# Modulation sums spread over other stages, and other banks for one inverse, in a two-layer hybrid decoder trunk

## The chip, the cores and the metric

The kernel runs on one core of a Trainium2 chip. The metric is the device time of one execution in microseconds, from start to end; the median of several executions counts. Inputs and outputs are in the chip's memory, all in 32-bit floats.

## The reference

Two layers work on 256 tokens of width 2048. Each layer first makes six modulation rows from the condition `c`, then a mixer (half the width is sliding-window attention, half an RWKV-7 recurrence), then a SwiGLU feed-forward; both end in a layer norm.

```python
for l in range(DEPTH):
    mod = einsum('bd,de->be', silu(c), w_ada[l]) + b_ada[l]
    sh_m, sc_m, gt_m, sh_f, sc_f, gt_f = rows 0 to 5 of mod
    u = x * (1 + sc_m) + sh_m
    proj = u @ w_in[l]
    y_attn = sliding_window_attention(...)
    y_rwkv = rwkv7_group(...)
    x = layer_norm(alpha * x + gt_m * (concat(y_attn, y_rwkv) @ w_out[l]))
    u = x * (1 + sc_f) + sh_f
    gate, up = split(u @ w_gate_up[l])
    x = layer_norm(alpha * x + gt_f * ((silu(gate) * up) @ w_down[l]))
```

In the recurrence a state S of 64 by 64 per head follows `S = S*w + (S a) b' + v k'`, and the output is `S r`.

## The kernel before

**Weights.** All large products run in 32-bit floats rounded for TensorE, each weight split into a high and a low part, so that a product takes three matmuls. `steps` (line 364) streams a weight matrix: one DMA puts 1024 columns into a `raw` buffer (4 of them), ScalarE casts it to `hi` (line 380), VectorE subtracts to get `lo` (line 381, two buffers), and `stream` or `tstream` does the matmuls (lines 402 to 405, 414 to 416). One such step is 512 KB. All DMAs of the kernel are issued by one queue, SP's, in order.

**Modulation.** The product of `silu(c)` with `w_ada` is no matmul: `ada_steps` (line 244) makes half a row (1024 columns) in 16 steps. Each loads 512 KB of `w_ada` into an `ast` buffer (two of them, line 253), and VectorE adds it, scaled, to the sum `aacc` (line 257; the first of the 16 is line 255). Then TensorE transposes the sum in 8 blocks (line 277), ScalarE sums them, and a gate's half row (rows 2 and 5) is transposed once more and written to memory. Layer 0's first two rows are made ahead of everything; the other 20 half rows come from one generator, `ada_rest`, in a fixed order: 2, 4 and 3, 5 of layer 0; 1 and 0, 2, 4 and 3, 5 of layer 1. Here one of its 16 additions is called a modulation step.

**What sets when a modulation step comes.** Three kinds of numbers advance the generator. `pump`, called once per weight step, advances it by a pace: `AP` in the mixer, `AO` from the output projection to the first part of the feed-forward, `AF_` behind that, each with one number per layer. `recur` advances it by `AR` at each of four chunks. The operations of the attention (`a`, `b`, `c`) advance it by `AA` each. Where a row is needed and not there, `need` runs the generator until it is. Before the change 18 of the 20 half rows are begun in layer 0; the last two, row 5 of layer 1, which the last gate needs, fall into the second mixer.

**The mixer.** Eight pairs of heads are worked on in four recurrent groups of two. For group g the order string `ORDER[l]` (line 36) lists: `D` decays, `R` projection, `A` preparation, `I` the inverse of a triangular matrix, `C` the recurrence over four chunks, `E` closing; then the attention (`Q` its projection, `a` rotation, `b` weights, `c` gathering) and the output projection's first 1024 columns (`w`, `z`). The inverse (`invert`, line 722) goes through memory: GpSimd inverts 16 by 16 blocks, which are written to `tinv` and read back as `tm`; then two levels merge blocks, each with a transpose on VectorE (line 745), matmuls into a bank `m1` (line 749), a masked multiply `yx` (line 752), matmuls into `m2` (line 756) and an addition (line 757).

**Banks.** `bank` (line 88) gives out PSUM banks: tag `cb` is a ring of two, used by the recurrence (line 760) and the closing (line 836); tag `mb` alternates between `m0` and `m1`, one bank each, used by the preparations, the transposes and the modulation sums. Four more banks, `acc`, hold products and the attention.

**Order on the engines.** The program is written in the order of these strings and calls. A scheduler then lays every engine's instructions out by its own estimate of time, and each engine takes its list in order. Changed numbers of `AP` to `AF_` so move instructions everywhere behind the first place they touch, not only the modulation steps.

## Time and profile before

| | |
|---|---|
| median of three executions | 2698.06 us (2688.91 to 2700.31) |
| the profiled execution | 2694.28 us |
| its span, first to last instruction | 2692.6 us |
| mean granted clock of TensorE | 0.965 |
| busy in the span: TensorE, VectorE, ScalarE, GpSimd | 93%, 68%, 44%, 5% |
| moved by DMA | 637.49 MB, mean 237 GB/s |

The engines are named PE (TensorE), PEld (its weight loads), DVE (VectorE), ACT (ScalarE), POOL (GpSimd) and SP (the engine that issues DMAs). A busy time is the time in which at least one instruction of the engine ran. A wait is the idle time of an engine before an instruction, put down to the instruction or DMA that came last before it. L257 is line 257. A tile's name, as `aacc<-ast,cond,aacc`, gives what is written and what is read. The clock is the share of 2.4 GHz that was granted to TensorE. Layer 0's mixer lies at about 135 to 600 us, its feed-forward up to 1400; layer 1's mixer from 1446 to about 1860, its feed-forward behind that.

### The profile page before, as it was taken

How to read it: one execution, taken by the hardware profiler on the slowest of the kernel's cores; microseconds unless marked ns; L12 is line 12 of the kernel's file. 1: busy time of each engine (PE TensorE's matmuls, PEld its weight loads, DVE VectorE, ACT ScalarE, POOL GpSimd, SP SyncE). 2: the span in 40 equal slices, each digit the busy share in tenths (PEclk: the TensorE clock that was granted, in tenths of full speed). 3: DMA queues.
4: the chain of work that ended last, by engine and by line, in shares of the span. 5: the costliest groups of instructions: out<-in, count | busy, mean ns of one | idle time of the engine just before them, and what ended most of it. 6: DMA issues, size and time to landing. Idle time of an engine off the chain costs nothing.

```text
span 2692.6 us, 41752 instructions
## 1 busy us (share of the span) xinstructions
PE 2501.1 (93%) x15325; PEld 2093.1 (78%) x15325; DVE 1841.0 (68%) x2469; ACT 1188.3 (44%) x2029; POOL 135.0 (5%) x355
## 2 busy tenths in 40 slices
PE   3788998788999999999999999979899999999997
PEld 2687886567888888888889877867688888888887
DVE  6866767979877777777788677555764545545456
ACT  2364452435444444444445544534444444344442
POOL 1002112000000000000000022110000000000000
PEclk9789998899999999999999999989999999999999
DMA  9968668688998888889878586424756656666654
GB/s 315 381 188 253 198 191 238 180 317 296 353 330 309 297 303 312 293 295 308 308 263 304 174 259 188 117 72 144 253 172 188 190 186 196 195 189 189 193 188 149
DMA packets 351999, 637.49 MB, mean 237 GB/s; under 512 B 75894, under 2 KB 142898, under 8 KB 350258
## 3 DMA queue, kind: packets, MB, share of 16 engines
q1 hardware_dynamic: 351794, 634.82, 71.6%
q8 instruction: 120, 1.97, 0.3%
q14 instruction: 85, 0.70, 0.1%
HBM read 622.08 MB, written 12.62 MB: 236 GB/s over the span
## 4 chain that ended last, share of the span: by engine, by line
PE 68%; DMA 8%; DVE 6%; ACT 2%; issue 1%; POOL 1%; SPq 0%; DVEq 0%; POOLq 0%; ACTq 0%
PE acc L403 19%; PE acc L402 19%; PE acc L405 19%; DMA ast<-in_w_ada_dram 3%; DVE aacc L257 2%; PE acc L414 2%; PE acc L415 2%; PE acc L416 2%; DVE lo L381 1%; DMA raw<-in_w_gate_up_dram 1%; PE mb L1225 1%; DMA raw<-in_w_out_dram 1%; DMA yf<-yd 1%; PE mb L277 1%; ACT pr L947 0%
## 5 line engine op out<-in xcount | busy, mean ns | idle before, releaser
L380 ACT CAST hi<-raw 128x1024 fp32r<-128x1024 f32 (+2 forms) x728 | 758.5, 1044 | 1110.8 <-PE acc L405 833.1
L381 DVE TENSOR_TENSOR lo<-raw,hi 128x1024 fp32r<-128x1024 f32 (+2 forms) x728 | 880.2, 1212 | 519.8 <-PE acc L403 347.1
L403 PE MATMUL acc<-lo,u 128*128 128x512 f32 x1568 | 513.4, 395 | 11.9 <-DVE lo L381 11.8
L405 PE MATMUL acc<-hi,u 128*128 128x512 f32 x1568 | 505.8, 391 | 0.0
L257 DVE SCALAR_TENSOR_TENSOR aacc<-ast,cond,aacc 128x1024 f32<-128x1024 f32 x300 | 384.1, 1280 | 127.8 <-DMA ast<-in_w_ada_dram 126.6
L402 PE MATMUL acc<-hi,u 128*128 128x512 f32 x1568 | 457.2, 393 | 0.9 <-ACT u L360 0.5
L403 PEld LDWEIGHTS acc<-lo,u 128*128 128x128 f32 x1568 | 293.8, 189 | 76.4 <-DVE lo L381 16.2
L402 PEld LDWEIGHTS acc<-hi,u 128*128 128x128 f32 x1568 | 294.9, 188 | 63.4 <-ACT sg L1218 0.9
L405 PEld LDWEIGHTS acc<-hi,u 128*128 128x128 f32 x1568 | 295.2, 188 | 61.8 <-issue 0.5
L403 PE MATMUL acc<-lo,ht 128*128 128x512 f32 (+1 forms) x720 | 243.6, 377 | 3.0 <-DVE lo L381 2.9
L405 PE MATMUL acc<-hi,ht 128*128 128x512 f32 (+1 forms) x720 | 242.2, 375 | 0.0
L414 PE MATMUL acc<-u,hi 128*128 128x256 f32 x720 | 206.1, 293 | 14.0 <-ACT hi L380 14.0
L402 PE MATMUL acc<-hi,ht 128*128 128x512 f32 (+1 forms) x720 | 217.0, 376 | 0.0
L415 PE MATMUL acc<-u,hi 128*128 128x256 f32 x720 | 204.5, 291 | 0.0
L416 PE MATMUL acc<-u,lo 128*128 128x256 f32 x720 | 193.1, 294 | 7.1 <-DVE lo L381 7.1
L403 PEld LDWEIGHTS acc<-lo,ht 128*128 128x128 f32 x720 | 135.0, 188 | 29.3 <-DVE lo L381 5.6
L414 PEld LDWEIGHTS acc<-u,hi 128*128 128x128 f32 x720 | 141.9, 197 | 19.3 <-ACT hi L380 14.9
L405 PEld LDWEIGHTS acc<-hi,ht 128*128 128x128 f32 x720 | 135.6, 188 | 24.2
L402 PEld LDWEIGHTS acc<-hi,ht 128*128 128x128 f32 x720 | 134.8, 188 | 24.4
L415 PEld LDWEIGHTS acc<-u,hi 128*128 128x128 f32 x720 | 141.7, 197 | 2.6 <-issue 1.6
L416 PEld LDWEIGHTS acc<-u,lo 128*128 128x128 f32 x720 | 133.8, 197 | 11.6 <-DVE lo L381 9.0
L1067 POOL TENSOR_TENSOR brs<-brs,mhalf 128x1 f32<-128x1 f32 x8 | 7.6, 955 | 1698.7 <-DVE brs L1066 772.1
(349 smaller groups left out, 2901.1 us busy)
## 6 DMA issues: line engine op xcount, KB each, us to landing
ast<-in_w_ada_dram SPq DMA_DIRECT2D x368, 512.0 KB
raw<-in_w_gate_up_dram SPq DMA_DIRECT2D x704, 256.0 KB
raw<-in_w_down_dram SPq DMA_DIRECT2D x176, 512.0 KB
raw<-in_w_in_dram SPq DMA_DIRECT2D x82, 512.0 KB
raw<-in_w_out_dram SPq DMA_DIRECT2D x64, 512.0 KB
raw<-in_w_in_dram SPq DMA_DIRECT2D x120, 256.0 KB
ast<-in_w_ada_dram SPq DMA_DIRECT2D x32, 256.0 KB
lnw<-in_ln_w_dram SPq DMA_DIRECT2D x4, 1024.0 KB
```

Source lines behind the costliest of these rows:

```text
L257: ins = V.scalar_tensor_tensor(acc, t, cond[:, j:j + 1], acc, ALU.mult, ALU.add)
L277: PE.transpose(b[:, i * P:(i + 1) * P], blocks[q + i], ident)
L380: S.copy(h, fl)
L381: ins = V.tensor_tensor(r, fl, h.bitcast(F32), ALU.subtract)
L402: PE.matmul(bt, lhsT=xh, rhs=hi[:, c0:c0 + w], start=st, stop=False)
L403: PE.matmul(bt, lhsT=xh, rhs=lo[:, c0:c0 + w], start=False, stop=False)
L405: PE.matmul(banks[t][q][:, 0:w], lhsT=xl, rhs=hi[:, c0:c0 + w], start=False, stop=sp_)
L414: PE.matmul(bt, lhsT=hi[:, c0:c0 + w], rhs=xh, start=st and opens, stop=False)
L415: PE.matmul(bt, lhsT=hi[:, c0:c0 + w], rhs=xl, start=False, stop=False)
L416: PE.matmul(bt, lhsT=lo[:, c0:c0 + w], rhs=xh, start=False, stop=sp_ and closes)
L1067: G.tensor_tensor(rs[:, 0:1], rs[:, 0:1], mhalf[:, 0:1], ALU.pow)
L1225: PE.transpose(b[:, i * T + t * P:i * T + (t + 1) * P], hh[t][:, (2 * k2 + i) * P:(2 * k2 + i + 1) * P], ident)
```

## The change

Layer 1's numbers fall: no modulation step comes from the recurrence (7 before) or the attention (45), the mixer's pace goes from 0.3 to 0.2 and that from the output projection on from 2.9 to 0. Layer 0's feed-forward goes from 0.75 to 0.8. And the four merge banks of the inverse of the fourth recurrent group of layer 1 come from `mb` in place of `cb`.

```diff
--- before.py
+++ after.py
@@ -46,13 +46,13 @@
 LAG = 2
 WB = (4, 3, 2)
 RED = 1
-AR = (3, 7)
-AA = (1, 45)
-AP = (0.65, 0.3)
-AO = (1.1, 2.9)
-AF_ = (0.75, 0.55)
+AR = (3, 0)
+AA = (1, 0)
+AP = (0.65, 0.2)
+AO = (1.1, 0.0)
+AF_ = (0.8, 0.55)
 COEX = (0, 0)
-IB = 'cb'
+IB = (('cb',) * 4, ('cb', 'cb', 'cb', 'mb'))
 EB = 'cb'
 CE = (0, 1, 0, 0)
 NE = (1,)
@@ -743,14 +743,14 @@
             for level in range(2):
                 yt = pb.tile([P, 2 * NCH, CH], F32, tag="ytr", name="ytr", bufs=1)
                 V.transpose(yt.rearrange("p e s -> p (e s)"), tm.rearrange("p e s -> p (e s)"))
-                m1 = bank("m1", IB)
+                m1 = bank("m1", IB[l][g])
                 for e in range(2 * NCH):
                     for i in I2:
                         PE.matmul(m1[BH[i], e * CH:(e + 1) * CH], lhsT=st[i]["am"][e // NCH][BH[i], e % NCH, 0:CH], rhs=yt[BH[i], e, :],
                                   start=True, stop=True)
                 yx = pb.tile([P, 2 * NCH, CH], F32, tag="yx", name="yx", bufs=1)
                 V.tensor_mul(yx, m1.rearrange("p (e s) -> p e s", s=CH), mmask[:, level:level + 1, :].to_broadcast([P, 2 * NCH, CH]))
-                m2 = bank("m2", IB)
+                m2 = bank("m2", IB[l][g])
                 for e in range(2 * NCH):
                     for i in I2:
                         PE.matmul(m2[BH[i], e * CH:(e + 1) * CH], lhsT=yx[BH[i], e, :], rhs=tm[BH[i], e, :], start=True, stop=True)
```

**First place: VectorE in the second mixer**, around an inverse's second step. `bv` ends a preparation, `lw` and `ar` belong to decays and preparation, `xk` and `xr` to the shifted projections, `ytr` is the inverse's transpose. Before (here from the third group's preparation, around the second group's inverse):

```order
L455 SCALAR_TENSOR_TENSOR xk<-acc,par_132,xk 128x255
L257 SCALAR_TENSOR_TENSOR aacc<-ast,cond,aacc 128x1024
L720 TENSOR_TENSOR bv<-bnb,vx 128x256
L662 SCALAR_TENSOR_TENSOR ar<-xk,der_134,e_15512 128x4x64
L381 TENSOR_TENSOR lo<-raw,hi 128x1024
L455 SCALAR_TENSOR_TENSOR xr<-acc,par_132,xr 128x255
L257 SCALAR_TENSOR_TENSOR aacc<-ast,cond,aacc 128x1024
L662 SCALAR_TENSOR_TENSOR ar<-xk,der_134,e_15525 128x4x64
L745 STREAM_TRANSPOSE ytr<-tm 128x512
L455 SCALAR_TENSOR_TENSOR xr<-acc,par_132,xr 128x255
L675 TENSOR_TENSOR ar<-xr,e_15512 128x4x64
```

Now, around the transpose of the first group's inverse:

```order
L662 SCALAR_TENSOR_TENSOR ar<-xk,der_134,e_14424 128x4x64
L720 TENSOR_TENSOR bv<-bnb,vx 128x256
L611 MEMSET e_15901 128x4
L745 STREAM_TRANSPOSE ytr<-tm 128x512
L455 SCALAR_TENSOR_TENSOR xr<-acc,par_132,xr 128x255
L381 TENSOR_TENSOR lo<-raw,hi 128x1024
L675 TENSOR_TENSOR ar<-xr,e_14424 128x4x64
L611 MEMSET e_15914 128x4
L381 TENSOR_TENSOR lo<-raw,hi 128x1024
L752 TENSOR_TENSOR yx<-m_14757,mmask 128x512
```

The modulation steps that stood between these instructions are gone from this stretch; the `lo` splits follow each other more closely. In the whole mixer 32 steps of lines 255 and 257 stood behind the first value-residual instruction (line 545); now 9 stand there, 2 behind the coefficients of the next part (line 1089) and 9 in the feed-forward.

**Second place: VectorE at the layer norm that ends layer 0.** `tp` is the feed-forward's last piece times its gate, `z` the residual stream, `bst`, `bmv` and `brs` its statistics; lines 1264 to 1267 and 1064 to 1078 are done once per half of the tokens. Before:

```order
L1264 TENSOR_TENSOR tp<-acc,gtf 128x512
L1265 SCALAR_TENSOR_TENSOR z<-z,tp 128x512
L1267 BN_STATS bst<-z 128x6
L1064 BN_AGGR bmv<-bst 128x2
L1066 TENSOR_SCALAR brs<-bmv 128x1
L1072 SCALAR_TENSOR_TENSOR brs<-bmv,brs 128x1
L1078 TENSOR_SCALAR z<-z,brs 128x512 x2
L1264 TENSOR_TENSOR tp<-acc,gtf 128x512
L1265 SCALAR_TENSOR_TENSOR z<-z,tp 128x512
L1267 BN_STATS bst<-z 128x6
L1064 BN_AGGR bmv<-bst 128x2
L1066 TENSOR_SCALAR brs<-bmv 128x1
```

Now (ahead of the first row stand line 1264 and one more modulation step):

```order
L257 SCALAR_TENSOR_TENSOR aacc<-ast,cond,aacc 128x1024
L1265 SCALAR_TENSOR_TENSOR z<-z,tp 128x512
L1267 BN_STATS bst<-z 128x6
L1064 BN_AGGR bmv<-bst 128x2
L1066 TENSOR_SCALAR brs<-bmv 128x1
L1264 TENSOR_TENSOR tp<-acc,gtf 128x512
L1072 SCALAR_TENSOR_TENSOR brs<-bmv,brs 128x1
L1265 SCALAR_TENSOR_TENSOR z<-z,tp 128x512
L1078 TENSOR_SCALAR z<-z,brs 128x512 x2
L257 SCALAR_TENSOR_TENSOR aacc<-ast,cond,aacc 128x1024
L1267 BN_STATS bst<-z 128x6
L257 SCALAR_TENSOR_TENSOR aacc<-ast,cond,aacc 128x1024
```

One step stood ahead of the chain. Now three stand in it, one of them before the first half's line 1265 and two around the second half's statistics. On the DMA queue the four loads that feed these and the next step stand in one row, where single ones stood between the weights.

**Third place: TensorE at the attention's start in the second mixer.** `qr` is the rotated query, `ob` and `db` are the third group's recurrence, `m` is a merge bank of the fourth inverse, `qT` enters the attention's scores. Before:

```order
L906 MATMUL acc<-ident,qr 128x128 x3
L825 MATMUL db<-state_13876,mt 64x64
L906 MATMUL acc<-ident,qr 128x128 x2
L811 MATMUL ob<-state_13875,rh 64x128 x2
L814 MATMUL ob<-uv,am 64x64 x4
L749 MATMUL m_17408<-ytr,am 64x64 x7
L906 MATMUL acc<-ident,qr 128x128
L749 MATMUL m_17408<-ytr,am 64x64
L906 MATMUL acc<-ident,qr 128x128 x3
L749 MATMUL m_17408<-ytr,am 64x64 x2
L906 MATMUL acc<-ident,qr 128x128 x2
L925 MATMUL acc<-qT 128x256 x4
```

Now:

```order
L906 MATMUL acc<-ident,qr 128x128 x4
L811 MATMUL ob<-state_13932,rh 64x128 x2
L814 MATMUL ob<-uv,am 64x64 x4
L845 MATMUL gb<-gda,g2a 128x256
L846 MATMUL gb<-gdb,g2b 128x256
L845 MATMUL gb<-gda,g2a 128x256
L846 MATMUL gb<-gdb,g2b 128x256
L906 MATMUL acc<-ident,qr 128x128 x2
L749 MATMUL m_17347<-ytr,am 64x64 x16
L906 MATMUL acc<-ident,qr 128x128 x6
L925 MATMUL acc<-qT 128x256 x4
L756 MATMUL m_17366<-tm,yx 64x64 x7
```

The first merge's 16 matmuls, which stood in four pieces between the transposes of `qr`, now stand in one.

## Rows read from the trace of the kernel before

**Rows 1.** Busy us (count) by stage of PE, PEld, DVE, ACT, POOL; clock, DMA share, GB/s.
```profile
650.00:1340.00 690.00, 685.37 (x3102) 563.73 (x3101) 525.17 (x502) 317.28 (x478) 0.00 (x0) 1.00 0.89 309
1446.00:1655.00 209.00, 194.52 (x1695) 169.79 (x1695) 151.13 (x218) 105.19 (x211) 30.36 (x68) 0.97 0.74 232
1655.00:1764.00 109.00, 108.18 (x1159) 91.15 (x1160) 63.67 (x110) 48.97 (x95) 22.37 (x65) 0.98 0.47 128
1764.00:1830.00 66.00, 48.97 (x520) 37.01 (x522) 43.13 (x164) 28.64 (x104) 2.79 (x5) 0.82 0.18 52
1950.00:2620.00 670.00, 670.00 (x3012) 555.10 (x3011) 341.44 (x341) 283.58 (x310) 0.00 (x0) 1.00 0.59 189
```

**Rows 2.** The same view, line 257 alone: DVE busy us (count), clock, DMA share, GB/s.
```profile
650.00:1340.00 690.00, 190.48 (x149) 1.00 0.89 309
...
1446.00:1655.00 209.00, 47.38 (x37) 0.97 0.74 232
```

**Rows 3.** Waits of VectorE, 1446 to 1655 us: total, times, longest.
```profile
DVE aacc L257 <- DMA ast<-in_w_ada_dram: 28.9, 16, 6.9
```

**Rows 4.** Timeline of VectorE at the three places: start, length, instruction, idle before it.
```profile
1568.95 1.28 DVE L257 SCALAR_TENSOR_TENSOR aacc<-ast,cond,aacc 128x1024 f32<-128x1024 f32 x1 [4.93 <-DMA ast<-in_w_ada_dram]
...
1585.85 1.28 DVE L257 SCALAR_TENSOR_TENSOR aacc<-ast,cond,aacc 128x1024 f32<-128x1024 f32 x1 [3.35 <-DMA ast<-in_w_ada_dram]
...
1650.65 1.28 DVE L257 SCALAR_TENSOR_TENSOR aacc<-ast,cond,aacc 128x1024 f32<-128x1024 f32 x1 [6.86 <-DMA ast<-in_w_ada_dram]
...
1654.12 1.22 DVE L381 TENSOR_TENSOR lo<-raw,hi 128x1024 fp32r<-128x1024 f32 x1
```

**Rows 5.** Waits of TensorE, 1560 to 1655 us.
```profile
PE ab L599 <- DVE e L611: 3.0, 1, 3.0
PE acc L403 <- DVE lo L381: 2.2, 1, 2.2
```

**Rows 6.** Timeline of TensorE behind the last of the three.
```profile
1655.39 0.80 PE L403 MATMUL acc<-lo,u 128*128 128x512 f32 x1 [5.32 <-DVE lo L381]
...
1657.27 0.63 PE L402 MATMUL acc<-hi,u 128*128 128x512 f32 x1
1657.69 0.63 PE L403 MATMUL acc<-lo,u 128*128 128x512 f32 x1
...
1658.93 0.39 PE L403 MATMUL acc<-lo,u 128*128 128x512 f32 x1
1659.16 0.39 PE L405 MATMUL acc<-hi,u 128*128 128x512 f32 x1
```

**Rows 7.** Timeline of the DMA queue ahead of the last of the three.
```profile
1645.00 1.29 SPq L738 DMA_DIRECT2D tinv<-ttl  x2
1646.38 0.57 SPq L253 DMA_DIRECT2D ast<-in_w_ada_dram  x1
```

**Rows 8.** The view of rows 1 for two stretches at the lower granted clock.
```profile
1587.20:1594.00 6.80, 6.48 (x47) 5.30 (x48) 4.63 (x9) 1.93 (x7) 0.00 (x0) 0.50 0.97 342
...
1788.60:1805.60 17.00, 15.51 (x114) 11.61 (x115) 12.30 (x60) 8.85 (x37) 0.00 (x0) 0.50 0.00 0
```

**Rows 9.** Waits of TensorE, 1400 to 1690 us, the layer norm's.
```profile
PE mb L354 <- DVE z L1078: 4.0, 1, 4.0
```

**Rows 10.** Waits of TensorE and of VectorE in feed-forward 0.
```profile
PE acc L403 <- DVE lo L381: 3.9, 7, 1.2
...
DVE aacc L257 <- DMA ast<-in_w_ada_dram: 60.0, 48, 3.6
```

**Rows 11.** The view of rows 1 for the slice with the most bytes in feed-forward 0.
```profile
673.00:740.30 67.30, 66.23 (x298) 53.89 (x297) 55.00 (x55) 32.41 (x50) 0.00 (x0) 1.00 0.97 353
```

**Rows 12.** Waits of TensorE, 1690 to 1960 us, the attention's and the inverse's.
```profile
PE acc L906 <- DVE qr L899: 6.0, 1, 6.0
PE acc L925 <- DVE mx L932: 5.1, 1, 5.1
...
PE m L749 <- DVE es L942: 0.3, 1, 0.3
```


## The prediction

> **What bounds the kernel now.** I read the busy time of each engine by stage first. In the feed-forward of layer 0 (650 to 1340 us) TensorE is busy 685.37 of 690 us, in that of layer 1 (1950 to 2620) 670 of 670 [rows 1]: these stages are TensorE's, and work put on another engine there costs only what makes TensorE wait. The second mixer is different. In its first part (1446 to 1655 us) TensorE is busy 194.52 of 209 us, in its second part (1655 to 1764) 108.18 of 109, in the attention at its end (1764 to 1830) 48.97 of 66. What is to be seen: the first part loses 14.5 us, the second 0.8.
>
> The second view splits off the modulation steps, VectorE's multiply-adds of line 257: 37 stand in the first part and 149 in layer 0's feed-forward [rows 2]; the last of all starts at 1650.65 [rows 4], so the second part has none. The third view, of waits, says what they do in the first part: 16 of the 37 hold VectorE until their piece of `w_ada` lands, 28.9 us in all, 6.9 the longest [rows 3]. VectorE works in order, so all that stands behind such a step waits too. The timelines show three places where TensorE pays. At 1568.95 a step starts after 4.93 us of idle VectorE, and the `lo` split behind it releases TensorE after 2.2 us. At 1585.85 one starts after 3.35 us, the `bv` multiply behind it reads a preparation bank, and TensorE's next decay matmul has waited 3.0 us (the releaser named is a tiny instruction behind the multiply). At 1650.65 one starts after 6.86 us, the `lo` split comes at 1654.12, and TensorE has stood 5.32 us [rows 4 to 6]. The cause of the last lies on the DMA queue: it wrote the inverse's result, `tinv`, at 1645.00, and the step's load, which stands behind that write, left at 1646.38 [rows 7].
>
> **The change part by part.** Total work is the same: 20 half rows of 16 modulation steps, some of which move on VectorE and in the DMA queue, and their sums with them. By the order of the program 32 steps (two opening ones of line 255 among them) stand behind the first value-residual instruction of layer 1 before, and 9 of them before the output projection now. Of the other 23, 12 go ahead into layer 0's feed-forward and the start of the second projection, 2 to the output projection, 9 to layer 1's feed-forward.
>
> *Taken out of the second mixer.* The three stalls are 2.2 + 3.0 + 5.32 = 10.5 us. After a stall TensorE's clock stays at its lower level, 1.2 of 2.4 GHz, for a while: after the last one, matmuls of 512 columns follow each other every 0.42 us, and every 0.23 once it is back [rows 6], so 45% of the time is lost. TensorE worked so from 1655.39 to 1658.93, which loses 1.6 us. From 1587.20 to 1594.00, behind the middle stall, the granted clock is 0.50 with TensorE busy 6.48 of 6.80 us [rows 8], which loses 2.9 at the most. I take 10.5 + 4.5 = 15.0 us out. Bounds: 9.1, if the middle stall and its clock stay because the inverse and the decay matmuls wait for something else there, and 17.5, if all but what the second part shows of the 14.5 us goes: 209 x 0.8 / 109 = 1.5 would be left, 13.0 saved, and the 4.5 of the clock with it come on top.
>
> *Left in it.* Nine steps remain in the mixer and two in the output projection. Priced as those of before, 15.0 / 37 = 0.41 us each, they cost 11 x 0.41 = 4.5 us. Bounds: 0, if none has to wait, and 10.5 if they fall on such places again.
>
> *The layer norm between the layers.* Three steps now stand inside its chain on VectorE, where one stood ahead of it (second place of the order). A step takes 1.28 us and the next instruction starts 1.2 us after it [rows 4]. TensorE already waits 4.0 us there for `z` [rows 9], so nothing covers them: 3 x 1.2 = 3.6 us at the most, less a little, since a multiply now fills the wait for GpSimd's power; I take +3.5. Their loads are four in a row on the DMA queue, each needing one of two buffers. Bounds: 0, if the first falls in time in which TensorE still multiplies, and 3.6 + 4.93 + 6.86 = 15.4, if two of them wait as the two longest above.
>
> *Layer 0's feed-forward.* It holds 12 steps more. TensorE lost 3.9 us there to the `lo` splits with 149 steps [rows 10], so 12 x 3.9 / 149 = 0.3 us. VectorE is busy 525 of 690 us [rows 1], 15 us more fits. Bounds 0 and 35 (the last rival). The HBM Reference of the Trainium skill, Specifications (TRN2), speaks against it: it gives a core an effective 358 GB/s, and the busiest slice here already moves 353 [rows 11]. Scaled by 318 / 309 for the 12 loads of 0.52 MB that slice would want 363, and by the page it would last 1.4%, some 0.9 us, longer. The rows of this trace decide otherwise: at 353 GB/s TensorE was busy 66.23 of 67.30 us.
>
> *Layer 1's feed-forward.* Nine steps of 1.28 us and one half row's sum (9 transposes) fall into 670 us in which VectorE is busy 341 and the DMA engines 59% [rows 1]. Nothing waits there now. I take 0; if the cover were gone, one wait as the longest seen, 5.3 us.
>
> *The banks of the fourth inverse.* In layer 1 its four merges take the two banks of the preparations in place of the ring that the recurrence and the closing use. Its matmuls lose 0.3 us to waits now [rows 12], so I price the swap by that. On TensorE the first merge now stands in one piece between the query transposes, where it stood in four (third place of the order). The end of the attention is set by other waits: 6.0 us for the rotated query and 5.1 us for the masked maximum, both VectorE's [rows 12], and those chains are not touched. I take 0; bounds -16 (rival below) and +6, one more wait like the longest.
>
> **Sum.** -15.0 + 4.5 + 3.5 + 0.3 = -6.7 us against the profiled execution, which took 2694.28 us: 2687.6, called **2688**. That execution lies 3.8 us under the median of the runs shown, 2698.06 (2688.91 to 2700.31). What a measurement of this kernel can tell from no change is about 0.5%, 13.5 us, so "faster" begins at 2684.6. The likeliest case alone reaches from 2681 (all stalls gone, layer norm cheap) to 2696 (steps left wait again).
>
> **The rivals.**
> *The attention shortens too.* If the fourth inverse was held by its banks, its merges end earlier, the last recurrence moves ahead, and the end of the mixer closes up. Price: half of the 17.0 us that TensorE idles from 1764 to 1830, 8.5, and the long stretch at the lower clock (1788.60 to 1805.60, busy 15.51 us [rows 8]), 45% of it, 7.0: 2688 - 15.5 = 2672.5. For it: the changed order puts the first mask of that inverse ahead of the last rotations, and the last recurrence ahead of the last softmax. Against: the waits there name VectorE's attention chain, not a bank. The Trainium skill, Trainium Kernel Development and Optimization, Best Practices, says that consistent bubbles can mean that PSUM ran out. By that rule these bubbles are the bank's and 2672.5 is the time; no row here ends on a bank, so it keeps a chance of 0.23.
>
> *The wait only moves.* The three steps in the layer norm find their loads late, as the step at 1650.65 did, and the layer norm costs the 15.4 us of its upper bound in place of the 3.5 taken: 2688 + 11.9 = 2700. For it: four loads in a row with two buffers. Against: eleven other instructions stand on VectorE between the step that frees a buffer and the first that needs its load there (second place of the order), and in the worst case shown a load took 4.3 us from its issue (1646.38) to its step's start (1650.65). Chance 0.18.
>
> *Slower: the denser steps break layer 0's feed-forward.* There 48 steps wait 60.0 us in all for their loads, 3.6 the longest, and TensorE hardly notices [rows 10]. The wait of 4.93 us cost TensorE 2.2, so the splits made ahead cover about 2.7 us; from there on each further microsecond is TensorE's. If the added loads push every third of those 48 to 4.93, that is 16 x 2.2 = 35 us: 2688 + 35 = 2723. For it: the DMA engines are busy 89% of that stage [rows 1]. Against: 97% in the busiest slice did not do it [rows 11]. Chance 0.12.
>
> *It does not do what it says* is excluded by the order: the steps have left the mixer.
>
> **How the numbers follow.** The likeliest case has the remaining 0.47, of which 0.15 lies under 2684.6. Faster: 0.15 + 0.23 and 0.02 for a moved wait that still leaves a gain, 0.40. Slower: 0.12 and 0.01 of the moved wait's far end, 0.13. Within 0.5%: 0.47. The range takes in the likeliest case, the first rival to 2669 and the moved wait up to 2705, and leaves out the slower rival and the tails.
>
> **What would show it.** Right: in the second mixer TensorE's waits for `lo` of 2.2 and 5.3 us and for the decay matmul are gone, line 257 waits there a few microseconds in place of 28.9, the part up to the second group's recurrence is busy as the part after it was (99%); in the layer norm the wait for `z` is 7 to 8 us in place of 4.0; both feed-forwards keep their length within 2 us. Wrong: waits for `lo` in layer 0's feed-forward over 10 us; a wait for `z` over 12; new waits of several microseconds in the mixer with no modulation step ahead of them, which would say that the order, not the steps, sets them; an attention part that is shorter or longer than 66 us by over 5.

## The result and the profile after

The changed kernel takes 2699.51 us, median of 20 executions (2692.76 to 2707.12), against 2693.85 (2682.87 to 2700.44) of the kernel before on the same chip. The ratio is 1.0019, 95% interval 1.0010 to 1.0028: slower by 0.19%, 5 us, where I forecast 6.7 us faster. That is less than the 0.5% that I had set as the bound of "no change", but it lies on the slow side, and the interval leaves out 1. The profiled execution took 2697.74 us, span 2696.0.

The view of busy time by stage, after; columns as in [rows 1]:

```profile
650.00:1340.00 690.00, 681.79 (x3076) 557.53 (x3075) 533.16 (x511) 315.72 (x475) 0.00 (x0) 1.00 0.90 313
1446.00:1655.00 209.00, 201.04 (x1818) 177.14 (x1817) 137.11 (x224) 108.91 (x195) 26.40 (x72) 0.98 0.61 184
1655.00:1764.00 109.00, 107.93 (x1100) 90.53 (x1098) 63.61 (x102) 51.32 (x99) 14.00 (x47) 1.00 0.54 159
1764.00:1830.00 66.00, 53.39 (x554) 40.01 (x553) 42.68 (x163) 24.92 (x87) 7.29 (x23) 0.77 0.14 36
1950.00:2620.00 670.00, 669.32 (x3012) 554.16 (x3011) 351.02 (x349) 285.88 (x327) 0.00 (x0) 1.00 0.60 194
```

The first part of the second mixer is filled, as forecast: TensorE busy 201.04 of 209 us, 194.52 before. But the feed-forward of layer 0 has lost 3.6 us of busy time in the same 690 us. Its waits, of TensorE and then of VectorE, 650 to 1346 us:

```profile
PE acc L403 <- DVE lo L381: 7.9, 12, 1.2
...
DVE aacc L257 <- DMA ast<-in_w_ada_dram: 72.1, 62, 3.5
```

TensorE waits for `lo` 12 times where it did 7 times, 7.9 us for 3.9; the steps wait for loads 62 times, 72.1 us, for 48 and 60.0 [rows 10]. The longest wait is the same. In the layer norm between the layers, TensorE's waits for `z`, by its timeline, and the stretch at the lower clock that begins within the second, by the view of busy time:

```profile
1411.02 0.44 PE L354 MATMUL mb<-ident,z 128*128 128x128 f32 x2 [2.34 <-DVE z L1078]
1416.46 1.54 PE L354 MATMUL mb<-ident,z 128*128 128x128 f32 x6 [5.00 <-DVE z L1078]
```

```profile
1413.80:1424.10 10.30, 7.05 (x30) 5.94 (x31) 6.79 (x16) 7.32 (x14) 0.54 (x1) 0.50 0.47 151
```

2.34 + 5.00 = 7.3 us for the 4.0 of before [rows 9]. The clock is at 1.2 GHz for 10.3 us from the second of these waits on, TensorE busy 7.05 us of it; before, the trace has 6.8 us at that clock (1406.30 to 1413.10).

**Stage by stage.** To compare kernels I cut every trace at the same instructions: A, the 2000th matmul on streamed weights (655 us in the kernel before); B, the start of the last transpose of a hidden row in layer 0's feed-forward (L1225); D, the first matmul of layer 1's value residual (L530); E, the first transpose of a rotated query (L906); G and H, the 7400th and 8000th streamed matmul, both in layer 1's feed-forward; and the last streamed matmul. A to B is layer 0's feed-forward; B to D the rest of its last product, the layer norm and the start of layer 1's projection; D to E the second mixer up to the attention; E to G the attention with what stands beside it, the output projection and its layer norm. In microseconds, one profiled execution each; "numbers" means layer 1's four:

| kernel | A to B | B to D | D to E | E to G | G to H | A to end | ratio to before |
|---|---|---|---|---|---|---|---|
| before | 637.5 | 185.9 | 295.7 | 214.6 | 138.8 | 2023.6 | |
| the change | 643.3 | 192.4 | 283.8 | 215.3 | 139.9 | 2025.9 | 1.0019 |
| e1, pace back | 638.6 | 187.6 | 292.3 | 214.3 | 140.9 | 2024.9 | 1.0001 |
| e2, banks alone | 637.9 | 185.7 | 295.2 | 208.7 | 138.8 | 2017.4 | 0.9962 |
| e3, pace alone | 646.3 | 189.4 | 312.5 | 220.0 | 138.8 | 2058.2 | 1.0136 |
| e4, banks back | 643.5 | 189.9 | 297.7 | 217.8 | 139.9 | 2039.9 | 1.0042 |
| e13, numbers alone | 639.7 | 186.2 | 288.1 | 215.0 | 140.9 | 2021.1 | 1.0005 |
| e5, no step in mixer | 638.1 | 187.7 | 280.1 | 215.1 | 141.7 | 2014.9 | 0.9969 |
| e9, pace 0.3 in mixer | 637.6 | 186.3 | 290.4 | 214.8 | 139.9 | 2020.1 | 0.9981 |
| e8, pause in norm | 647.5 | 186.8 | 283.2 | 213.5 | 142.5 | 2024.7 | 0.9985 |
| e10, 0.85, pause | 644.5 | 188.4 | 290.9 | 210.8 | 139.9 | 2025.6 | 1.0002 |
| e14, banks of two | 638.9 | 188.6 | 287.9 | 220.0 | 138.8 | 2025.3 | 0.9996 |
| e15, quarter of the work | 640.2 | 185.6 | 287.4 | 215.8 | 139.9 | 2020.1 | |
| e16, quarter of the loads | 634.2 | 185.3 | 279.0 | 211.4 | 139.9 | 2000.9 | |
| f1, pace 0.70 | 632.3 | 187.1 | 288.0 | 219.1 | 140.5 | 2019.2 | 0.9975 |
| f3, steps in output | 640.7 | 187.0 | 280.7 | 271.4 | 138.8 | 2069.7 | 1.0159 |

By the two profiles the change gained 295.7 - 283.8 = 11.9 us in the mixer up to the attention, and lost 5.8 in layer 0's feed-forward, 6.5 between the layers, 0.7 from the attention to G and 1.1 in the next feed-forward: +2.2 us net (2025.9 - 2023.6 is 2.3, with rounding). The part ahead of A is the same program and took 1.1 us longer.

**What one execution of a stage is worth.** Over single stages many rows hold the same instructions in the same order, up to an instruction or two, and so repeat each other. From A to B the eight kernels at pace 0.75 are one program: 637.5 to 640.7 us, mean 638.6. The four at 0.80 (the change, e3, e4 and, with a few instructions of VectorE in other places, e8) took 643.3 to 647.5, mean 645.2. From B to D the first eight took 185.7 to 188.6, mean 186.9; the change, e3 and e4 189.4 to 192.4, mean 190.5. From D to E the kernel before and e2 are one program (295.7 and 295.2), e1 and e13 another (292.3 and 288.1), and the change and e4 a third: 283.8 and 297.7. These last two differ by 13.9 us without any edit in the stage. Most of it lies at one place. TensorE's timeline and the view of busy time there, of e4 first and then of the change:

```profile
1691.48 1.22 PE L784 MATMUL mr<-bkt,ah 64*128 64x128 f32 x4 [2.66 <-ACT ah L778]
1691.30:1715.20 23.90, 23.72 (x117) 18.81 (x118) 5.85 (x12) 7.22 (x20) 6.57 (x28) 0.50 0.14 35
```

```profile
1685.90 0.71 PE L784 MATMUL mr<-bkt,ah 64*128 64x128 f32 x4 [1.07 <-ACT ah L778]
1685.90:1709.90 24.00, 24.00 (x248) 20.81 (x249) 8.93 (x16) 13.54 (x39) 7.01 (x28) 1.00 0.31 85
```

In e4 TensorE waited 2.66 us, and then 117 matmuls took 23.9 us at 1.2 GHz; in the change it waited 1.07, the clock stayed, and 24 us held 248. So a few us between two single executions of this mixer say little. By the means of each program's executions the change gained 295.5 - 290.8 = 4.7 us there, not 11.9, and lost 6.5 in layer 0's feed-forward and 3.7 between the layers. With the 0.7 and 1.1 that is +7.3 us, against the 5 of the medians; the mixer's 4.7 is an estimate from two pairs, and could be 7 off.

### The profile page after: what moved, and what is told of

Its sections match the earlier page's. It is cut to its first block, busy times and chain, and to the rows that moved or that the text cites. A ratio compares the mean times of both kernels' runs of the same rounds, so it can differ in the third digit from the quotient of the medians.

```text
span 2696.0 us, 41746 instructions
## 1 busy us (share of the span) xinstructions
PE 2507.1 (93%) x15325; PEld 2093.3 (78%) x15325; DVE 1840.1 (68%) x2469; ACT 1189.5 (44%) x2029; POOL 125.4 (5%) x355
## 5 line engine op out<-in xcount | busy, mean ns | idle before, releaser
L306 DVE SCALAR_TENSOR_TENSOR aacc<-ast,cond,aacc 128x1024 f32<-128x1024 f32 (+1 forms) x75 | 80.2, 1070 | 12.3 <-DMA ast<-in_w_ada_dram 10.5
```

The lines of the kernel that those rows point to most:

```text
L306: V.scalar_tensor_tensor(acc, t[:, j], cond[:, j0 + j:j0 + j + 1], acc, ALU.mult, ALU.add)
```

## The experiments

My theory at the start: the mixer's gain is real, and it was given back by the denser steps of layer 0's feed-forward and by those in the layer norm. The rivals: the scheduler's new layout, and the banks.

**e1, pace back.**

```diff
-AF_ = (0.8, 0.55)
+AF_ = (0.75, 0.55)
```

> The changed kernel with layer 0's feed-forward pace put back from 0.8 to 0.75; the lower numbers of layer 1 and the banks stay. Theory (the second mixer gained about 12 us; it was given back in layer 0's feed-forward, about 5, and in the layer norm and projection between the layers, about 6.5): both losses go and the gain stays, so 0.9955 to 0.997 of the kernel before, about 2684 us; TensorE waits for lo in layer 0's feed-forward 4 us in all (7.9 with the change), for z in the layer norm 4 (7.3 with the change), and the second value stage starts about 1479 to 1481 us, in place of 1492. Rival 1 (the new layout of the second mixer and its banks, not the pace, cost the time): 1.000 to 1.003 of the kernel before, as the change itself. Rival 2 (the 12 us gain belongs to the early steps, which now fall on the mixer again): the mixer keeps stalls for lo of 2 us and more and the ratio is 0.999 to 1.001.

Measured 1.0001 (0.9989 to 1.0012), 2693.95 us. Both losses went: 638.6 and 187.6, wait for `z` 4.0. So the pace accounts for the 5 us by which the change is slower (1.0019 - 1.0001). But the time did not fall to 2684, and the ratio is that of the rivals: what is left of the change, lower numbers and other banks, gives nothing in the time as a whole. The mixer took 292.3 us, 3.4 less than before. The stalls of before are gone, and another has come. TensorE, VectorE and the DMA queue around the first inverse, in their timelines:

```profile
1577.52 1.32 PE L749 MATMUL m<-ytr,am 64*64 64x64 f32 x18 [5.25 <-DVE ytr L745]
```

```profile
1576.75 0.71 DVE L745 STREAM_TRANSPOSE ytr<-tm 128x512 f32<-128x512 f32 x1 [7.91 <-DMA tm<-tinv]
```

```profile
1569.84 1.28 SPq L738 DMA_DIRECT2D tinv<-ttl  x2
1572.72 1.28 SPq L741 DMA_DIRECT2D tm<-tinv  x2
```

The inverse's blocks are written at 1569.84, read back at 1572.72, and the transpose starts at 1576.75: 6.9 us through memory, which VectorE stood idle for 7.91 and TensorE for 5.25. With fewer steps ahead of it the first merge stands at 1577.52, where the kernel before has it at 1590.2, and TensorE has no product left to cover the way. VectorE waited for this read-back in the kernel before too; its waits from 1446 to 1860 us there:

```profile
DVE ytr L745 <- DMA tm<-tinv: 9.8, 3, 4.9
```

The products behind it hid that: TensorE's wait for the transpose does not appear there among those of [rows 5] and [rows 12]. The new wait goes with the order of the instructions: it is 5.2 us in e1 and in e13, and 2.1 in the change and in e4.

**e2, banks alone**: the kernel before, with `IB` of the change.

> The kernel before with only the banks of the fourth inverse changed. Theory: the banks cost and give nothing that can be told, 0.999 to 1.001 of the kernel before (2691 to 2697 us), and the attention from its first merge to the last gathering lasts 68 to 71 us. Rival (the swap is what costs: preparation banks held by merges hold up what else uses them): 1.002 to 1.005, with a new wait of 2 us or more on a bank in the tail of the second mixer. Rival (the swap shortens the tail): 0.994 to 0.998.

Measured 0.9962 (0.9952 to 0.9973), 2685.05 us: about 10 us faster by the ratio (6.2 from A to the end in one profile), the largest gain of any single edit, from the one that I had priced at 0. It is in E to G, 208.7 for 214.6. TensorE's timeline where the third group's recurrence ends:

```profile
1770.66 1.85 PE L749 MATMUL m<-ytr,am 64*64 64x64 f32 x30 [3.12 <-DVE ytr L745]
1773.85 0.48 PE L906 MATMUL acc<-ident,qr 128*128 128x128 f32 x1 [1.33 <-DVE qr L899]
```

and its waits from 1650 to 1940 us:

```profile
PE acc L906 <- DVE qr L899: 1.3, 1, 1.3
PE acc L925 <- DVE mx L932: 0.3, 1, 0.3
```

With its own banks the merge's first matmuls need not stand behind the recurrence's use of the ring. They run in the hole ahead of the rotated query, after a wait of 3.1 us for their transpose; the query's wait falls from 6.0 to 1.3 us, and that for the masked maximum from 5.1 to 0.3 [rows 12]. The merge's masked multiply (L752) starts at 1782.55, and at 1789.31 in the kernel before. No wait in [rows 12] named a bank; the bank stood in the order that the scheduler wrote, and the trace showed only what TensorE did next.

**e3, pace alone**: the kernel before, with `AF_ = (0.8, 0.55)`.

> The kernel before with only layer 0's feed-forward pace raised from 0.75 to 0.8. Theory: the losses come with it, +5 us in layer 0's feed-forward and +6 between the layers, and part of the gain too, since some of the steps leave the second mixer's first part: 1.001 to 1.005 of the kernel before (2697 to 2707 us); waits for lo in layer 0's feed-forward 7 to 9 us, for z 7 to 8 us. Rival (the pace is harmless and the layout of the second mixer cost the time): 0.996 to 1.000, waits for lo there 4 us.

Measured 1.0136 (1.0121 to 1.0151), 2731.34 us, far worse than any theory had it. The losses in layer 0's feed-forward (+8.8) and between the layers (+3.5) are there. The larger part, 16.8 and 5.4 us, is in the mixer and behind it, where the mean granted clock from D to E was 0.92 (0.97 before). With the rows begun earlier each step there falls at another place; which of them costs so much is not shown. TensorE's waits there, 1446 to 1940 us:

```profile
PE acc L906 <- DVE qr L899: 10.1, 1, 10.1
PE m L749 <- DVE ytr L745: 9.0, 3, 4.6
```

**e4, banks back**: the change without its `IB`.

> The changed kernel with the banks of the fourth inverse put back; all paces as changed. Theory: as the changed kernel within 2 us, 1.001 to 1.003 of the kernel before. Rival (the banks cost the time): 0.996 to 0.999. The attention part tells it too: 71.0 us from its start to the last gathering with the change, 68.6 before; theory 68.5 to 71 either way.

Measured 1.0042 (1.0026 to 1.0057), 2706.6 us, above what either theory had. So the banks give the change some 6 us: 1.0042 - 1.0019 = 0.0023. The theory that they do nothing has fallen twice. D to G lasts 495.2 to 507.1 us in the eight kernels with these banks and all of the sums (f3 apart), 503.1 to 532.5 in the four without (before, e3, e4, e13); the two overlap.

**e13, numbers alone**: the kernel before with layer 1's lower numbers.

```diff
-AR = (3, 7)
-AA = (1, 45)
-AP = (0.65, 0.3)
-AO = (1.1, 2.9)
+AR = (3, 0)
+AA = (1, 0)
+AP = (0.65, 0.2)
+AO = (1.1, 0.0)
```

> The kernel before with only layer 1's four numbers lowered (no steps from recurrence and attention, mixer pace 0.2, 0 from the output projection on); pace 0.75 and the old banks stay. This is the term that the prediction put at -10.5 us, by itself. Prediction's theory: the stalls go and nothing takes their place, 0.996 of the kernel before (about 2684 us), and the stretch from the second value stage to the end of the output projection is 10 us shorter than before. Rival (the denser order runs into the next thing, the inverse's read-back through memory and, without the changed banks, the ring of the recurrence): 0.998 to 1.003, with waits of 3 us or more before an inverse's first merge; the stretch is within 6 us of before.

Measured 1.0005 (0.9993 to 1.0016). D to E fell by 7.6 us, with the same wait of 5.2 for the inverse's read-back as e1; G to H took 2.1 back. The 2.2 us more from A to B are no cost of the edit, since the program there is that of the kernel before. D to G is 7.2 us shorter, between the two; the time as a whole is the rival's.

**e5 and e9, how many steps stay in the mixer**: e1 with `AP = (0.65, 0.0)` and `(0.65, 0.3)`: 0 and 16 steps in its weight stream, where e1 has 9.

> The kernel with pace back (0.75 in layer 0's feed-forward, all other numbers of the change) and layer 1's mixer pace at 0 instead of 0.2: all 32 steps of the last row fall into layer 1's feed-forward, none into the second mixer. Theory (with the steps gone, the first part of the second mixer is set by the inverse's read-back through memory, which the denser order reaches earlier): no gain over the run with pace back, 0.998 to 1.002 of the kernel before, and a wait of 3 us or more before an inverse's first merge (L749, for ytr) stays or comes at another inverse. Rival (the steps left still cost 0.41 us each): 9 x 0.41 = 3.7 us faster than the run with pace back, about 0.9987 of the kernel before, and the wait before the merge goes.

> The same kernel with pace back, layer 1's mixer pace at 0.3 instead of 0.2: 16 steps stand in the mixer's weight stream instead of 9, nothing comes from the recurrence or the attention. Theory (the layout decides, not the count of steps): the time differs from the run with pace back by as much as any re-layout does, up to 10 us either way, without order in the count 0, 9, 16. Rival (each step costs 0.41 us): 7 x 0.41 = 2.9 us slower than the run with pace back, 1.001 of the kernel before.

Measured 0.9969 (0.9958 to 0.9981) and 0.9981 (0.9969 to 0.9993). By the medians the ratio is 0.9969 with 0 steps, 1.0001 with 9 and 0.9981 with 16: no line through the count, so a price of 0.41 us per step does not hold. D to E, 280.1, 292.3 and 290.4, shows none either, but these are single executions. With no step, this mixer runs 262.8 us without a fall of the clock, in the view of busy time:

```profile
1493.80:1756.60 262.80, 260.99 (x2575) 221.95 (x2574) 150.84 (x257) 129.38 (x231) 42.26 (x133) 1.00 0.48 136
```

My theory missed e5: it said no gain over e1, and there is one of 0.3%. The wait for the read-back did come, at a later inverse (5.8 us, behind 1650), as it also said.

**e8 and e10, a pause in the layer norm**: the change, with the generator stopped from the last columns of layer 0's last product to the end of the layer norm; e10 has pace 0.85 besides.

```diff
             for c0, w in ((0, 1024), (1024, 512), (1536, 512)):
                 nq = w // 512
+                if c0 == 1536 and not first and l == 0:
+                    pace[0] = 0.0
...
+        pace[0] = AF_[l]
         us = []
         feeds = front(l + 1, us, inputs(fp, z, l, "ln2_w", "ln2_b", l + 1, 1, 0, us))
```

> The changed kernel with its generator paused from the last columns of layer 0's last product to the end of the layer norm. Pace 0.8 stays for the rest of the feed-forward. Theory (two separate losses): layer 0's feed-forward keeps its loss (waits for lo 7 to 9 us, last hidden transpose 5 to 7 us later than before), the wait for z falls back from 7.3 to 4.0 us, the lower clock behind it from 10.2 to 6.8, and the second value stage starts at 1483 to 1486 us, between 1478.6 of before and 1492.0 of the change. Rival (the steps in the layer norm are not what makes z late): wait for z 7 us still, start at 1490 or later.

> The paused kernel with pace 0.85 instead of 0.8 in layer 0's feed-forward: about 12 steps more in it again. Theory (density of steps is what costs there): waits for lo in that stage grow beyond the 8 us of pace 0.8, to 12 us or more, and the last hidden transpose comes 11 us or more later than in the kernel before. Rival (what costs at 0.8 are a few chance meetings, not density): waits for lo 4 to 9 us, transpose 2 to 8 us late.

Measured 0.9985 (0.9974 to 0.9997) and 1.0002 (0.9991 to 1.0013). TensorE's waits in e8, in the feed-forward and in the layer norm:

```profile
PE acc L403 <- DVE lo L381: 12.2, 17, 1.3
...
PE mb L354 <- DVE z L1078: 4.0, 1, 4.0
```

The two losses are two: with the pause the wait for `z` is 4.0 again and B to D 186.8, while A to B keeps its loss (647.5). The pause makes the whole 9 us faster than the change (1.0019 - 0.9985), more than the wait for `z` accounts for; where the rest comes from is not shown. Two details missed: the stretch at the lower clock stayed 10.2 us, and the second value stage starts at 1487.6, since the feed-forward lost 10 us and not 6, with the change's program. e10 is a miss of mine: with 165 steps in the 690 us (158 in the change) the waits for `lo` were 7.0 and the stage 644.5, not longer.

**e14, banks of two groups**: the kernel before with

```diff
-IB = 'cb'
+IB = (('cb',) * 4, ('cb', 'cb', 'mb', 'mb'))
```

> The kernel before with the merges of the third and the fourth inverse of layer 1 (not the fourth alone) on the preparations' banks. Theory (the recurrence's ring of two held the merges of the last inverse, and so the attention at the end): the third inverse stands amid products that fill such holes, so a second group brings little: 0.994 to 0.999 of the kernel before, as with the fourth alone (0.996), and the end of the mixer is as short as there. Rival (any re-layout does that by chance): 0.999 to 1.006.

Measured 0.9996 (0.9984 to 1.0008), at the rival's end; E to G 220.0, no shorter than before. What helps for one group's merges was lost with two.

**e15 and e16, what of a step costs there.** Both are the change; e15 does the multiply-adds on 256 of 1024 columns, e16 loads 256 of 1024.

```diff
-                ins = V.scalar_tensor_tensor(acc, t, cond[:, j:j + 1], acc, ALU.mult, ALU.add)
+                ins = V.scalar_tensor_tensor(acc[:, 0:256], t[:, 0:256], cond[:, j:j + 1], acc[:, 0:256], ALU.mult, ALU.add)
```

```diff
-            t = adap.tile([P, 1024], F32, tag="ast", name="ast", bufs=2)
-            dma(t, src[:, j, n0:n0 + 1024])
+            t = adap.tile([P, 256], F32, tag="ast", name="ast", bufs=2)
+            dma(t, src[:, j, n0:n0 + 256])
...
+                V.scalar_tensor_tensor(acc[:, 256:1024], fixed[:, 256:1024], cond[:, j:j + 1], acc[:, 256:1024], ALU.mult, ALU.add)
+                ins = V.scalar_tensor_tensor(acc[:, 0:256], t, cond[:, j:j + 1], acc[:, 0:256], ALU.mult, ALU.add)
```

> The changed kernel with the multiply-adds of the modulation steps on 256 of their 1024 columns; the loads stay whole. Left out: three quarters of these sums, so the modulation rows are other ones. It asks what costs in layer 0's feed-forward at pace 0.8. Theory (the steps wait for their loads, in order on VectorE, and the split behind them comes late): shorter steps change little, the step's waits for loads stay at 60 us or more, waits for lo at 5 to 10, and the stage from the 2000th streamed matmul to the last hidden transpose stays at 642 to 648 us (637.5 before, 643.3 with the change). Rival (VectorE's own time is what is short): waits for lo under 3 us, 636 to 638 us.

> The changed kernel with the modulation steps' loads cut to 256 of 1024 columns; VectorE does the multiply-adds on all 1024, 768 of them from a constant tile, in two instructions. Left out: three quarters of these sums' data. Theory (loads): the steps' waits for loads fall under 15 us, waits for lo under 3 us, and the same stage lasts 635 to 638 us. Rival (VectorE's own time): waits for lo 5 us or more, 641 us or more, since VectorE has slightly more to do than in the change.

One execution each. The feed-forward in the view of busy time, and its waits, of e15 first and then of e16, whose line numbers stand 4 higher:

```profile
650.00:1340.00 690.00, 685.98 (x3092) 564.50 (x3091) 419.11 (x513) 317.59 (x480) 0.00 (x0) 1.00 0.90 317
```

```profile
PE acc L403 <- DVE lo L381: 3.7, 3, 2.7
...
DVE aacc L257 <- DMA ast<-in_w_ada_dram: 73.2, 60, 4.3
```

```profile
650.00:1340.00 690.00, 688.12 (x3119) 566.85 (x3118) 554.03 (x668) 320.67 (x485) 0.00 (x0) 1.00 0.71 222
```

```profile
PE acc L407 <- DVE lo L385: 1.6, 4, 0.6
...
DVE aacc L261 <- DMA ast<-in_w_ada_dram: 3.4, 6, 1.0
```

With 114 us less of VectorE's work the steps still wait 73.2 us for loads, but TensorE's waits for `lo` fall to 3.7 and the stage takes 640.2, between theory and rival and within what the kernels at 0.75 took. Of this some 5 us, by my estimate (2.73 and 45% of 6.07), lie at one wait and the lower clock around it, which the change's profile does not have:

```profile
655.63 1.22 PE L403 MATMUL acc<-lo,u 128*128 128x512 f32 x2 [2.73 <-DVE lo L381]
654.90:661.70 6.80, 6.07 (x17) 4.82 (x17) 5.50 (x10) 4.10 (x8) 0.00 (x0) 0.50 0.88 267
```

With the loads cut, VectorE has 21 us more to do than in the change, the waits fall to 3.4 and 1.6, and the stage takes 634.2, under all eight at 0.75. So VectorE's time by itself is not what is short (e16), and waits for loads by themselves do not make the loss either (e15): either cut takes it away. What fits both is a step that starts late and then holds VectorE for 1.28 us ahead of the split. The weights' own loads came earlier too with the others cut: ScalarE waited 52.8 us for them between A and B in the change, 10.5 in e16. That way to a late `lo` was not tested apart.

**f1, pace 0.70**: e1 with `AF_ = (0.7, 0.55)`.

> The kernel with pace back, with 0.70 instead of 0.75 in layer 0's feed-forward (12 steps fewer there; they go to the front and the mixer of layer 1). The stage from the 2000th streamed matmul to the last hidden transpose lasts 637.5 to 639.7 us at 0.75 in six profiles, 643.3 to 647.5 at 0.80 and 0.85 in five, and 634.2 with loads cut to a quarter. Theory (loads cost, and steeply near the top): 635 to 638 us, waits for lo under 4 us; three or four steps of the next half row now stand in the layer norm, so the wait for z is 6 to 8 us and the second value stage late by 3 to 4. Rival (chance layout): 639 us or more. In all 0.996 to 1.002 of the kernel before.

Measured 0.9975 (0.9964 to 0.9986). The stage takes 632.3 us, less than the 635 that I had as its floor, with 142 steps in the 690 us. The wait for `z` was 5.8, but the value stage was not late (187.1).

**f3, steps in the output projection**: e5 with `AO = (1.1, 2.9)`.

> The kernel with no step in the second mixer, with layer 1's pace behind the mixer at 2.9, as before the change, instead of 0: the 32 steps go to the output projection and the start of layer 1's feed-forward. Without them there, closing plus the first 600 matmuls of that feed-forward took 142.1 + 138.8 us (the kernel with the banks alone); with 32 steps spread over the feed-forward 148.4 + 141.7. Theory (the steps in the feed-forward's first part cost the 2.9 us, the closing's length comes from the layout of the tail): closing 144 to 150 us with L402 waiting for u 4 us or more, first part 139 to 142, 0.995 to 0.999 of the kernel before. Rival (the layer norm of layer 1 cannot take 11 steps at all): closing 152 us or more, 1.000 or more.

Measured 1.0159 (1.0144 to 1.0173), 2738.98 us: the rival. TensorE's wait, 1830 to 2150 us:

```profile
PE mb L277 <- DVE aacc L257: 34.2, 1, 34.2
```

The last half row's steps come in one burst in the layer norm, from 1938.71 to 1979.53 us on VectorE, and the transposes of its sum (L277) stand on TensorE ahead of the layer norm's own transposes: 34.2 us for a row that is needed only in the next stage.

## Why the prediction was wrong

**Layer 0's feed-forward: the first step that failed.** The prediction priced "12 x 3.9 / 149 = 0.3 us" for the added steps, with 0 to 35 around it. By the means of the same programs it measured 6.5, by the two profiles 5.8. Of the 12 steps 7 stand between A and B, the other 5 between B and D. By the modulation steps between A and B (lines 255 and 257) the stage took 632.3 us with 136 (pace 0.70, one execution), 638.6 on average with 147, 645.2 with 154, and 644.5 with 165 (one execution). From 136 to 147 and from 147 to 154 that is 0.6 and 0.9 us a step, over 20 times my 0.026, and behind that nothing more: no line, and no price per step that could be carried on.

I had taken the waits that a view names, 3.9 us, as all that steps cost there. TensorE's idle time from A to B (655.17 to 1292.71 us before, 656.33 to 1299.66 now) grew only from 4.6 to 7.2 us, 2.6 of the 5.8. By the distance from each matmul's start to the next's, without idle time, 0.5 lie in the transposes of one more half row's sum, 80 of line 277 for 72. The other 2.7 are in the streamed matmuls: 80 for 61 hold the engine 0.3 us or more, mostly the first behind a break, where the others take 0.23. That VectorE had room [rows 1] was true and beside the point. The slower rival had the mechanism, late loads that make `lo` late, at over five times the size that came; e15 and e16 fit loads and steps that do it together.

The page that I weighed there, the Trainium skill's HBM Reference, Specifications (TRN2), spoke for a loss, 0.9 us by its figure. The trace agrees with the direction: loads cut to a quarter took the loss away (e16). But 358 GB/s was the wrong figure to scale by. That section gives it as a core's share with both cores of a pair streaming, and says that a core streaming alone, as here, measures well above it, about 425. The trace agrees that it is no ceiling here: the second of the 40 slices of the profile's page of the change, ahead of 135 us, moved 382.

**The layer norm.** +3.5 forecast, and on average +3.7 measured between B and D; the +6.5 of the two profiles is its far end. The wait for `z` was right: 7.3 us for "7 to 8" in the change, 7.2 and 7.0 in e3 and e4. What I left out shows in the change's profile behind it: 3.4 us more at 1.2 GHz, at most 1.5 us, and 1.5 us more of waits in the start of the projection for `vx`, `u` and `lo`. Why `z` came late is shown by e8: without the steps in the chain the wait is 4.0.

**The second mixer: the second step that failed.** -10.5 forecast (15.0 out, 4.5 left). The -11.9 of the two profiles is luck and no proof: the same program took 297.7 us in e4. On average it is -4.7. All that was to be seen came: line 257 waits 1.4 us there for 28.9, no wait for `lo` over 1 us is left, the first part is 96% busy (99 forecast). But alone (e13) these numbers gave nothing in the time as a whole, 1.0005 (0.9993 to 1.0016), where 10.5 us would have been 0.9961. What failed is the term "15.0 us out": it took each stall away with nothing behind it. A new wait took the place of the old ones, 5.2 us for the inverse's read-back in e1 and e13, 2.1 in the change, which I had named nowhere: VectorE's transpose of `tm` had waited up to 4.9 us for it in the kernel before. My price of 0.41 us for a step that is left, 4.5 in all, failed too (e5 and e9).

**The banks.** 0 taken, with -16 as the bound and a rival that gave it 0.23. Alone they gave 10 us, in the change about 6. The rival's mechanism came in the run with the banks alone: the merges leave earlier, and the waits that named VectorE's attention chain shrank with them. In the change itself E to G was no shorter, 215.3 us for 214.6. The evidence against that rival, "the waits there name VectorE's attention chain, not a bank", was no evidence, since an engine that runs its list in order shows the wait of the instruction at the head, not of the one that the bank kept behind. The Trainium skill, Trainium Kernel Development and Optimization, Best Practices, says that consistent bubbles can mean that PSUM ran out; the run with the banks alone, 0.9962, fits that, though the bubbles were two single waits. That these banks are better in every layout is not so: e1 and e13 differ by nothing that can be told, and with two groups on these banks (e14) the gain was gone. So a new layout by chance is a rival to the ring for part of the 10 us, and no run excludes it.

**Layer 1's feed-forward.** 0 taken; it cost 1.1 us between G and H. That is not the 9 steps but the half row's sum: TensorE is never idle there in the kernel before and in the change, and its 9 transposes, 634 matmuls for 625, come on top. The change, e9 and e10 have one sum there with 9, 15 and 4 steps, and all took 139.9 us; e1 and e13 have two sums and 19 steps, and took 140.9. In e5 (24 steps, one sum) and e8 (16 steps, two sums) TensorE also stood idle, 1.6 and 1.3 us, and 141.7 and 142.5 went by. Work that I counted as covered was work of the engine that is full.

So the sum failed, on average, by 6.2 us in layer 0's feed-forward and 5.8 in the mixer (-4.7 for -10.5), by 0.2 between the layers, and by 0.7 and 1.1 behind: 14.0 us from -6.7 to +7.3, of which the medians show 12 (+5). The forecast's sign hung on two steps: small terms were priced by what the waits of before named, and the large one by the stalls that it removed.

**What stays open.** Why 0 and 16 steps in the mixer are faster than 9 is not shown; where the inverse's read-back falls is a candidate, but no run moved that alone. Which of a step's load and its length on VectorE costs more in layer 0's feed-forward is not known. Several kernels beat both: the banks alone, 2685.05 us (0.9962), and the banks with the last row wholly in layer 1's feed-forward (e5), 2686.29 (0.9969). They can't be told apart.

## What to carry to other kernels

Background work that moves from one stage to another is not priced by the waits that the taking stage shows. In a stage with TensorE full and the DMA engines busy 89%, 7 more loads, their steps and one more sum cost 6.5 us, where the waits of before came to 3.9 for all of them; with the DMA engines at 59%, 4 to 15 loads cost nothing that shows, and a sum the 1.1 us of TensorE that it takes. Before a difference between two profiles of a stage is read, look for two executions of one program in it: here they differed by 13.9 us. Where a scheduler lays out a list for each engine, the wait that a trace names is that of the instruction at the head; what a shared buffer kept behind it shows only when the buffer is changed. And a stall that is taken away is worth what lies between it and the next late thing, here a way through memory that already waited 4.9 us.

## What was not expected of the hardware

The same instructions took different times from one execution to the next. Ahead of A the program is that of the kernel before in every run but e15 and e16, and took between 648.1 us (e9) and 661.2 (e5). In e5 8.6 us of it come from one place; TensorE's timeline there:

```profile
317.20 0.63 PE L858 MATMUL oc<-ident,sq 128*128 128x128 f32 x4 [0.98 <-DVE sq L854]
320.27 0.80 PE L403 MATMUL acc<-lo,u 128*128 128x512 f32 x1 [2.44 <-DVE lo L381]
```

and the same stretch in the view of busy time, of e5 and then of the kernel before:

```profile
319.60:333.20 13.60, 12.93 (x68) 10.19 (x69) 11.44 (x22) 6.56 (x11) 0.00 (x0) 0.50 0.78 253
```

```profile
319.60:333.20 13.60, 13.60 (x146) 10.82 (x146) 13.60 (x27) 7.00 (x10) 0.00 (x0) 1.00 0.80 256
```

In the kernel before TensorE did not stand there at all. In e5 it stood 0.98 and 2.44 us, the granted clock fell to 1.2 GHz for 13.6 us with TensorE busy 12.93, and 68 matmuls went through where 146 had: 3.4 us of idle time cost 8.6. So a difference of 6 us between two kernels is not to be read from one execution of each. The stages are compared here from A on, which leaves this out, but the mixer from D to E has the same spread.
